# The first products of an encoder block on Trainium2: two beside the loading of x, or four

## Chip, core and metric

The kernel runs on one core of a Trainium2 chip. The metric is the device time of one execution in microseconds, taken as the median of several executions. TensorE (PE in the profile) multiplies, VectorE (DVE) and ScalarE (ACT) work on whole tiles of 128 partitions, GpSimd (POOL) can do such work too, and SyncE (SP) issues most transfers from main memory.

## What is computed

One layer of a bidirectional encoder, then a last norm, on 256 positions of width 2048. The start is all that matters here:

```python
h = rms_norm(x, norm1_g)           # x * rsqrt(mean(x*x) + eps) * g
proj = h @ w_in                    # 2048 -> 9632 columns
u_a, v_a, feat_b, gate_a, gate_b = split_cols(proj, ...)
y_a = sgu_mixer(u_a, v_a, ...)     # begins with gelu(v), gelu(u)
```

Behind it come a scan over 16 heads, two projections and a gated feed-forward part. All matrices are float32.

## The kernel before

x is held transposed: 16 tiles of 128 features x 256 positions, loaded two at a time into `xt` (256 KB each). The norm is applied late. Each tile of x is only multiplied by `norm1_g` (`split_scaled`, L176), and the products are multiplied by `rstd1` once it is known. For precision every operand is split into a rounded part and the rest: ACT writes the rounded part and DVE the difference. That holds for x (`h`, L177 on ACT and L178 on DVE, 128x256 each) and for the weights (`hl`, L223 and L224, 128x512 each).

The weights come as chunks: one load (`raw`, 256 KB) of four 128x128 tiles. A chunk costs one cast on ACT, one subtraction on DVE and eight matmuls, in four pairs of one 512-column and one 256-column matmul (L242, L246). A product over 2048 features is four chunks. A list of jobs says in which order the chunks run; `split_to` prepares a chunk, `load_to` issues loads, `advance` multiplies. Four `raw` buffers, four `hl` buffers and two banks of PSUM for products (`ps_mm`) are turned over, and a load is issued when the subtraction that read its buffer is done.

At the start `pair_up` interleaves the chunks of the first two products, so that each quarter of x is used for two products while the next one comes in (the loop at L479 to L486). In the same loop POOL squares x (L482) and DVE sums the squares (L484). A matmul with a matrix of ones (L490) then gives the sum over all features, from which DVE forms `rstd1` (L493 and `rsqrt`, seven small instructions). The products that wait for `rstd1` are held in `waiting` and passed to the Gelu afterwards. The vectors of all norms and scales come in one load, `colt` (184 KB, issued by ACT at L127), and the constants in another, `cst`; five small DVE instructions (L144 to L152) derive vectors from `colt` before anything else.

The order on each engine is the one in which the program issues its instructions, with small moves by the scheduler of the language.

Of the kernel before, what the change touches and what calls it, by code (L numbers as in the profile page):

```python
# [24 lines left out]
NP = RW // P  # L25
# [4 lines left out]
RK = 4  # L30
# [18 lines left out]
NFEAT = 4 + 3 * NP  # L49
# [8 lines left out]
COLS = {}  # L58
# [58 lines left out]
def hybrid_kernel(ctx: ExitStack, tc: tile.TileContext, xT, w_in, w_pa, w_pb, w_out, w_g, w_u, w_d,  # L117
                  cols, consts, lora, sgu_wT, sgu_b, out):
    nc = tc.nc
    V, A, PE, G = nc.vector, nc.scalar, nc.tensor, nc.gpsimd  # L120

    cpool = ctx.enter_context(tc.tile_pool(name="cpool", bufs=1))
    ps_mm = ctx.enter_context(tc.tile_pool(name="ps_mm", bufs=2, space=PSUM))
    ps_ms = ctx.enter_context(tc.tile_pool(name="ps_ms", bufs=1, space=PSUM))

    colt = cpool.tile([P, NCOLS], F32, name="colt")
    A.dma_start(colt, cols)  # L127
    cst = cpool.tile([P, NCONST], F32, name="cst")
# [12 lines left out]


    c0 = cpool.tile([P, NFEAT], F32, name="c0")
    V.tensor_tensor(out=c0, in0=colr("mu_p"), in1=colr("mu_n"), op=ALU.add)  # L144
    V.tensor_scalar(out=c0, in0=c0, scalar1=-1.0, scalar2=1.0, op0=ALU.mult, op1=ALU.add)
    wo, _ = COLS["w0_f"]
    hb = cpool.tile([P, 4 * NP], F32, name="hb")
    V.tensor_scalar(out=hb, in0=colt[:, wo:wo + 4 * NP], scalar1=0.5, scalar2=None, op0=ALU.mult)
    ka2 = cpool.tile([P, NP], F32, name="ka2")
    V.tensor_scalar(out=ka2, in0=colr("k_a"), scalar1=-1.0, scalar2=2.0, op0=ALU.mult, op1=ALU.add)  # L150
    rkh = cpool.tile([P, NP], F32, name="rkh")
    V.tensor_scalar(out=rkh, in0=colr("r_k"), scalar1=0.5, scalar2=None, op0=ALU.mult)  # L152
    nln2 = cpool.tile([P, 1], F32, name="nln2")
    V.memset(nln2, LN2)

# [3 lines left out]
    ones = con("ones")  # L159
# [16 lines left out]
    def split_scaled(dst, src, g):  # L176
        A.activation(dst[:, 0], src, AF.Copy, scale=g)  # L177
        V.scalar_tensor_tensor(out=dst[:, 1], in0=src, scalar=g, in1=dst[:, 0].bitcast(F32),  # L178
                               op0=ALU.mult, op1=ALU.subtract)


    jobs, raws, chunks = [], [], []
    ptr = dict(raw=0, hl=0, mm=0)
# [11 lines left out]
        jobs.append(job)  # L195
        return job

    def pair_up(n):

        order = [i + o for i in range(n) for o in (0, n)]  # L200
        at = {ri: i for i, ri in enumerate(order)}
        raws[:2 * n] = [raws[ri] for ri in order]
        first = sorted((c for c in chunks if c[1] < 2 * n), key=lambda c: at[c[1]])
# [12 lines left out]
    def split_to(i):  # L216
        while ptr["hl"] <= min(i, len(chunks) - 1):
            c = chunks[ptr["hl"]]
            load_to(c[1] + (pools["ahead"] if ptr["mm"] > 7 else 0))
            _, ri, s0, m, _ = c  # L220
            raw = raws[ri][3]
            hl = hl_p.tile([P, 2, HK, P], F32R, name="hl", tag="hl")
            A.copy(hl[:, 0, :m], raw[:, s0:s0 + m])  # L223
            V.tensor_tensor(out=hl[:, 1, :m], in0=raw[:, s0:s0 + m], in1=hl[:, 0, :m].bitcast(F32), op=ALU.subtract)  # L224
            c[4] = hl
            ptr["hl"] += 1

    def advance(n, ahead=HL_AHEAD):
        for _ in range(n):
            i = ptr["mm"]  # L230
            if i >= len(chunks):
                return
            split_to(i + ahead)
            job, ri, s0, m, hl = chunks[i]
            if job["ps"] is None:
                job["ps"] = ps_mm.tile([P, 512], F32, name="mm", tag="mm")
            ps = job["ps"]
            for j in range(m):
                k = raws[ri][1] + s0 + j
                a = job["act"](k)  # L240
                if job["wide"]:
                    PE.matmul(ps[:, 0:512], hl[:, 0, j], a.rearrange("p a t -> p (a t)"), start=(k == 0), stop=False)  # L242
                else:
                    PE.matmul(ps[:, 0:256], hl[:, 0, j], a[:, 0], start=(k == 0), stop=False)  # L244
                    PE.matmul(ps[:, 0:256], hl[:, 0, j], a[:, 1], start=False, stop=False)  # L245
                PE.matmul(ps[:, 0:256], hl[:, 1, j], a[:, 0], start=False, stop=(k == job["nk"] - 1))  # L246
            ptr["mm"] += 1
            if ptr["mm"] == job["last"]:
                job["done"](ps if job["wide"] else ps[:, 0:T])
# [12 lines left out]
    pools = dict(raw=ctx.enter_context(tc.tile_pool(name="raw", bufs=4)), ahead=2)  # L262
    hl_p = ctx.enter_context(tc.tile_pool(name="hl", bufs=4))
    ev = ctx.enter_context(tc.tile_pool(name="ev", bufs=2))
    drp = ctx.enter_context(tc.tile_pool(name="drp", bufs=1, space=bass.MemoryType.DRAM))
# [5 lines left out]
    h = [hp.tile([P, 2, T], F32R, name=f"h{k}") for k in range(KT)]  # L271
# [67 lines left out]
    ps_s = es_s.enter_context(tc.tile_pool(name="ps_s", bufs=2, space=PSUM))  # L339
# [7 lines left out]
    waiting = []  # L347

    def gelu(ps, outv, add):
        t = evac_sum(ev, ps)  # L350

        def then():
            V.tensor_tensor(out=t, in0=t, in1=rstd1, op=ALU.mult)
            A.activation(outv, t, AF.Gelu)
            if add == 0:
                A.copy(acc, outv)
            elif add is not None:
                V.tensor_tensor(out=acc, in0=acc, in1=outv, op=ALU.add)

        if waiting is None:  # L360
            then()
        else:
            waiting.append(then)
# [90 lines left out]
    def abreast(*gens):  # L454

        live = list(gens)
        while live:
# [5 lines left out]
                    live.remove(g)  # L463
            yield step

    pair_up(KT // RK)


    with tc.tile_pool(name="xin", bufs=1) as xin:
        XG = 2  # L470
        sq = [xin.tile([P, XG, T], F32, name=f"sq{g}") for g in range(KT // XG)]
        xt = [xin.tile([P, XG, T], F32, name=f"xt{g}") for g in range(KT // XG)]
        for g in range(KT // XG):
            nc.sync.dma_start(xt[g], xT[:, g * XG:(g + 1) * XG])
            if g % 2:
                load_to(g)
        load_to(8)
        nc.sync.dma_start(cst, consts)
        for g in range(KT // XG):  # L479
# [5 lines left out]
            if g % 2:  # L485
                advance(2, 1 if g < 7 else 0)  # L486
        advance(1, 1)
        sps = ps_ms.tile([P, 512], F32, name="ms", tag="ms")
        for j in range(XG):
            PE.matmul(sps[:, 0:T], ones, sq[0][:, j], start=(j == 0), stop=(j == XG - 1))  # L490
# [6 lines left out]
        waiting = None  # L497

    nc.sync.dma_start(wsT, sgu_wT)
    nc.sync.dma_start(bsb, sgu_b.to_broadcast([P, SW]))  # L500
    finish(last_v)
# [408 lines left out]
    for p in range(-1, NP):  # L910
# [12 lines left out]
        if p + 2 < NP:  # L923
            side.append((rwkv_rates(p + 2), RATES_Y))
            then.append((rwkv_operands(p + 2), OPER_Y))
        n = left() - (LAST if p == NP - 1 else 0)
# [11 lines left out]
                 ahead=RAW2 - 2)  # L938
# [82 lines left out]
    with tc.tile_pool(name="ev2", bufs=2, reuse_waits="tile") as ev2, \  # L1021
# [116 lines left out]
```

## Time and profile before

| | us |
|---|---|
| median of 3 runs | 1582.59 (1581.76 to 1582.97) |
| the profiled execution | 1567.25 |
| its span, first to last instruction | 1565.5 |
| PE busy in the span | 1531.2 (98%) |
| PE busy in the first 27 us | 15.14 |
| PE busy from 27 to 60 us | 33.00 |

All times of rows count from the start of the span. A row of a timeline gives the start, the length, engine, line, operation, output and inputs, the count of merged instructions, and in brackets the idle time of the engine before it with what ended that. Instructions of one engine overlap a little: a lone 128x512 subtraction is shown as 0.68 us, but two in a row start 0.60 us apart. So the cost in a full queue is read from starts, not from lengths. In the table of stretches the columns are busy time and instructions of each engine, then the granted clock, the share of the DMA engines in use, and GB/s.

### The profile page before, as it was taken

To read this page: it belongs to the slowest core of one execution; us is meant where nothing else is said; L and a number is where in the kernel's file an instruction comes from. 1 tells how busy PE (TensorE), PEld (TensorE's weight loads), DVE (VectorE), ACT (ScalarE), POOL (GpSimd) and SP (SyncE) were. 2 spreads that over 40 slices of the span, in tenths; PEclk is the share of its full clock that TensorE was granted. 3 is DMA by queue.
4 is the path that set the end of the run, shared out by engine and by line. 5 is a ranking of instruction groups with operands and counts; after the bars stand their busy time and mean duration, and the time that the engine had idled before them with its cause. 6 is when DMAs were issued, how large, how long until landed. Compare 5 with 4: busy or idle time off the path is not lost.

```text
span 1565.5 us, 35582 instructions
## 1 busy us (share of the span) xinstructions
PE 1531.2 (98%) x13420; PEld 1333.2 (85%) x13420; DVE 1222.2 (78%) x2500; ACT 922.6 (59%) x1920; POOL 37.9 (2%) x65
## 2 busy tenths in 40 slices
PE   6999999999999999999999999999999999999996
PEld 5888888888888878899998888888888888888885
DVE  8879998889898897687678777777787776555554
ACT  5667765665666655555556666666666665545452
POOL 2000000000000000000000000000000000000000
PEclk9999999999999999999999999999999999999998
DMA  6555553443443433597555555555555556666663
GB/s 230 195 181 177 166 160 126 132 144 120 135 140 116 139 100 124 161 316 240 187 182 188 194 190 189 189 192 190 190 189 189 190 191 191 189 191 190 190 190 100
DMA packets 151500, 273.72 MB, mean 175 GB/s; under 512 B 16928, under 2 KB 23200, under 8 KB 151328
## 3 DMA queue, kind: packets, MB, share of 16 engines
q1 hardware_dynamic: 148624, 263.91, 53.2%
q0 software_dynamic: 2560, 7.34, 1.4%
q8 instruction: 105, 1.72, 0.4%
q14 instruction: 67, 0.55, 0.1%
q10 hardware_dynamic: 144, 0.19, 0.0%
HBM read 265.09 MB, written 6.29 MB: 173 GB/s over the span
## 4 chain that ended last, share of the span: by engine, by line
PE 84%; issue 9%; DVE 4%; DMA 1%; ACT 1%; POOL 0%; SPq 0%; DVEq 0%; ACTq 0%; POOLq 0%
PE mm L242 45%; PE mm L246 26%; PE mm L244 3%; PE mm L245 3%; PE gp L669 1%; PE tp L717 1%; PE ms L541 1%; DVE hl L224 1%; DVE FQ L695 1%; PE tp L707 1%; PE cc L800 0%; DMA xt<-in_xT_dram 0%; PE tp L728 0%; DMA spill<-ev 0%; POOL spill L877 0%
## 5 line engine op out<-in xcount | busy, mean ns | idle before, releaser
L242 PE MATMUL mm<-h,hl 128*128 128x512 f32 x2624 | 935.7, 399 | 8.3 <-DVE h L178 7.6
L224 DVE TENSOR_TENSOR hl<-raw,hl 128x512 fp32r<-128x512 f32 x960 | 655.9, 689 | 231.0 <-ACT hl L223 227.3
L223 ACT CAST hl<-raw 128x512 fp32r<-128x512 f32 x960 | 594.7, 621 | 398.5 <-PE mm L246 284.9
L246 PE MATMUL mm<-h,hl 128*128 128x256 f32 x2624 | 733.3, 279 | 4.8 <-DVE hl L224 4.8
L242 PEld LDWEIGHTS mm<-h,hl 128*128 128x128 f32 x2624 | 493.2, 188 | 122.4 <-ACT hl L223 8.1
L246 PEld LDWEIGHTS mm<-h,hl 128*128 128x128 f32 x2624 | 495.0, 189 | 7.9 <-DVE hl L224 7.1
L242 PE MATMUL mm<-act,hl 128*128 128x512 f32 x660 | 228.8, 394 | 0.0
L246 PE MATMUL mm<-act,hl 128*128 128x256 f32 x704 | 195.3, 277 | 0.0
L242 PEld LDWEIGHTS mm<-act,hl 128*128 128x128 f32 x660 | 123.8, 188 | 28.7
L258 ACT COPY ev<-mm 128x256 f32<-128x256 f32 x180 | 67.1, 373 | 119.0 <-PE mm L246 118.7
L246 PEld LDWEIGHTS mm<-act,hl 128*128 128x128 f32 x704 | 132.4, 188 | 0.0
L259 DVE TENSOR_TENSOR ev<-mm,ev 128x256 f32<-128x256 f32 x180 | 75.9, 422 | 45.5 <-ACT ev L258 44.7
L246 PE MATMUL mm<-mg,hl 128*128 128x256 f32 x256 | 71.9, 281 | 0.0
L244 PE MATMUL mm<-mg,hl 128*128 128x256 f32 x256 | 71.7, 280 | 0.0
L245 PE MATMUL mm<-mg,hl 128*128 128x256 f32 x256 | 71.2, 278 | 0.0
L242 PE MATMUL mm<-ya,hl 128*128 128x512 f32 x128 | 48.2, 409 | 0.0
L244 PEld LDWEIGHTS mm<-mg,hl 128*128 128x128 f32 x256 | 48.1, 188 | 0.0
L245 PEld LDWEIGHTS mm<-mg,hl 128*128 128x128 f32 x256 | 48.1, 188 | 0.0
L246 PEld LDWEIGHTS mm<-mg,hl 128*128 128x128 f32 x256 | 48.1, 188 | 0.0
L1035 ACT ACTIVATE gt<-cp,colt 128x256 f32<-128x256 f32 x44 | 26.5, 603 | 19.1 <-DVE cp L1033 19.1
L246 PE MATMUL mm<-ybs,hl 128*128 128x256 f32 x128 | 36.2, 283 | 0.0
L245 PE MATMUL mm<-ybs,hl 128*128 128x256 f32 x128 | 36.2, 283 | 0.0
(285 smaller groups left out, 1523.6 us busy)
## 6 DMA issues: line engine op xcount, KB each, us to landing
raw<-in_w_in_dram SPq DMA_DIRECT2D x304, 256.0 KB, 3.0
raw<-in_w_g_dram SPq DMA_DIRECT2D x176, 256.0 KB, 3.1
raw<-in_w_u_dram SPq DMA_DIRECT2D x176, 256.0 KB, 2.9
raw<-in_w_d_dram SPq DMA_DIRECT2D x176, 256.0 KB, 2.9
raw<-in_w_out_dram SPq DMA_DIRECT2D x64, 256.0 KB, 3.0
raw<-in_w_pa_dram SPq DMA_DIRECT2D x32, 256.0 KB, 2.9
raw<-in_w_pb_dram SPq DMA_DIRECT2D x32, 256.0 KB, 4.7
spill<-ev POOLq DMA_DIRECT2D x32, 128.0 KB, 3.2
```

The source lines that it names most:

```text
L223: A.copy(hl[:, 0, :m], raw[:, s0:s0 + m])
L224: V.tensor_tensor(out=hl[:, 1, :m], in0=raw[:, s0:s0 + m], in1=hl[:, 0, :m].bitcast(F32), op=ALU.subtract)
L242: PE.matmul(ps[:, 0:512], hl[:, 0, j], a.rearrange("p a t -> p (a t)"), start=(k == 0), stop=False)
L244: PE.matmul(ps[:, 0:256], hl[:, 0, j], a[:, 0], start=(k == 0), stop=False)
L245: PE.matmul(ps[:, 0:256], hl[:, 0, j], a[:, 1], start=False, stop=False)
L246: PE.matmul(ps[:, 0:256], hl[:, 1, j], a[:, 0], start=False, stop=(k == job["nk"] - 1))
L258: A.copy(t, ps[:, 256:512])
L259: V.tensor_tensor(out=t, in0=ps[:, 0:256], in1=t, op=ALU.add)
L541: PE.matmul(ps[:, 0:T], bones, b[:, o], start=(o == 0), stop=(o == 1))
L669: PE.matmul(gps[hh][:, c * P:(c + 1) * P], BK[rows, d, c, hh:hh + 2, :].rearrange("p a b -> p (a b)"), AR[rows, d, c].rearrange("p a b -> ...
L695: V.copy_predicated(out=FQ2[qs, d, :, 1, :], mask=m2[qs, None, :].to_broadcast([32, NC, 32]), data=Gs[d][qs, q // 2, :, 0, b0:b0 + 32])
L1035: A.activation(gt, b[:, 1:T + 1], AF.Identity, scale=col("cw1", f), bias=col("cb", f))
```

## The change

Four products instead of two run side by side while x comes in. `line_up(4, 4)` takes the place of `pair_up(4)`; the third and fourth product borrow banks of PSUM (tags `sgt` and `sgm`) that are free until the gating stage. In this stage eight buffers (`rawx`) take the loads, and a load of a quarter of x is followed by the four chunks that use it. The squares are made by ACT, 128x512 each, in place of POOL; DVE still sums them. The scale of norm 1 comes in a load of its own (`g1t`, 16 columns), the whole `colt` only after half of x is in use, and the five small DVE instructions (`derive`) stand behind the norm. The matmul that sums the squares uses a matrix of ones made on the core (`on1`). Twelve 512-column matmuls of that constant by itself stand first on PE; nothing reads them. Results that wait for `rstd1` lie in four buffers (`evw`) instead of two.

```diff
+J0 = 4
+WARM = 12
...
+    g1t = cpool.tile([P, KT], F32, name="g1t")
+    A.dma_start(g1t, cols[:, 0:KT])
     colt = cpool.tile([P, NCOLS], F32, name="colt")
-    A.dma_start(colt, cols)
...
-    pair_up(KT // RK)
-
-
-    with tc.tile_pool(name="xin", bufs=1) as xin:
+    line_up(J0, KT // RK)
+
+
+    with tc.tile_pool(name="xin", bufs=1) as xin, tc.tile_pool(name="evw", bufs=J0) as evw, \
+            tc.tile_pool(name="rawx", bufs=2 * J0) as rawx:
...
+        warm = ps_ms.tile([P, 512], F32, name="ms", tag="ms")
+        for _ in range(WARM):
+            PE.matmul(warm, on1.bitcast(F32R), on1.bitcast(F32R)[:, None, :].to_broadcast([P, 4, P]), start=True, stop=True)
...
+        def squares(q):
+            for g in (2 * q, 2 * q + 1):
+                sn = sq if g == 0 else xin.tile([P, XG, T], F32, name="sn", tag="sn", bufs=2)
+                A.activation(sn, xt[g], AF.Square)
+                if g > 0:
+                    V.tensor_tensor(out=sq, in0=sq, in1=sn, op=ALU.add)
+
+        load_q(0)
+        load_q(1)
+        for q in range(NQ):
+            take(RK * q)
+            for i in range(J0):
+                c = J0 * q + i
+                split_to(c)
+                if i == 0:
+                    for k in range(RK * q + 1, RK * q + RK):
+                        take(k)
+                advance(1, 0)
+            load_q(q + 2)
+            if q == 1:
+                nc.sync.dma_start(colt, cols)
+            if q == NQ - 1:
+                pools["raw"] = main_raw
+                load_to(J0 * NQ + 2)
+            squares(q)
         nc.sync.dma_start(cst, consts)
-        for g in range(KT // XG):
-            for j in range(XG):
-                split_scaled(h[g * XG + j], xt[g][:, j], col("norm1_g", g * XG + j))
-            G.tensor_tensor(out=sq[g], in0=xt[g], in1=xt[g], op=ALU.mult)
-            if g > 0:
-                V.tensor_tensor(out=sq[0], in0=sq[0], in1=sq[g], op=ALU.add)
-            if g % 2:
-                advance(2, 1 if g < 7 else 0)
+        pools["ps"] = ps_next
         advance(1, 1)
```

What DVE does first, before the change (`h` are tiles of x, `hl` chunks of weights, `sq` sums of squares; the number behind a name tells tiles apart):

```order
L144 TENSOR_TENSOR c0_67<-colt_64 128x28
L148 TENSOR_SCALAR hb_70<-colt_64 128x32
L150 TENSOR_SCALAR ka2_72<-colt_64 128x8
L145 TENSOR_SCALAR c0_67<-c0_67 128x28
L152 TENSOR_SCALAR rkh_74<-colt_64 128x8
L178 SCALAR_TENSOR_TENSOR h0_100<-xt0_181,colt_64,h0_100 128x256
L178 SCALAR_TENSOR_TENSOR h1_101<-xt0_181,colt_64,h1_101 128x256
L178 SCALAR_TENSOR_TENSOR h2_102<-xt1_182,colt_64,h2_102 128x256
L178 SCALAR_TENSOR_TENSOR h3_103<-xt1_182,colt_64,h3_103 128x256
L224 TENSOR_TENSOR hl_227<-raw_191,hl_227 128x512
L224 TENSOR_TENSOR hl_230<-raw_193,hl_230 128x512
```

And with the change:

```order
L489 MEMSET on1_175 128x128
L185 SCALAR_TENSOR_TENSOR h0_96<-xt0_190,g1t_64,h0_96 128x256
L185 SCALAR_TENSOR_TENSOR h1_97<-xt0_190,g1t_64,h1_97 128x256
L231 TENSOR_TENSOR hl_221<-raw_200,hl_221 128x512
L185 SCALAR_TENSOR_TENSOR h2_98<-xt1_191,g1t_64,h2_98 128x256
L185 SCALAR_TENSOR_TENSOR h3_99<-xt1_191,g1t_64,h3_99 128x256
L231 TENSOR_TENSOR hl_239<-raw_203,hl_239 128x512
L517 TENSOR_TENSOR sq_198<-sq_198,sn_286 128x512
L231 TENSOR_TENSOR hl_251<-raw_205,hl_251 128x512
L231 TENSOR_TENSOR hl_263<-raw_207,hl_263 128x512
L185 SCALAR_TENSOR_TENSOR h4_100<-xt2_192,g1t_64,h4_100 128x256
```

The small vectors have left the front, the first chunk is prepared before the third tile of x, and four chunks instead of two follow each four tiles of x.

What DVE does where `rstd1` is formed (`ev` are products that wait for it, `ms` the sum over features), with the change:

```order
L266 TENSOR_TENSOR ev_477<-mm_266,ev_477 128x256
L231 TENSOR_TENSOR hl_552<-raw_496,hl_552 128x512
L545 TENSOR_SCALAR s1_513<-ms_510 128x256
L171 TENSOR_SCALAR rstd1_75<-s1_513 128x256
L174 TENSOR_TENSOR t1_514<-rstd1_75 128x256
L175 SCALAR_TENSOR_TENSOR t1_514<-t1_514,s1_513 128x256
L176 SCALAR_TENSOR_TENSOR rstd1_75<-t1_514,rstd1_75 128x256
L231 TENSOR_TENSOR hl_557<-raw_545,hl_557 128x512
L174 TENSOR_TENSOR t1_514<-rstd1_75 128x256
L231 TENSOR_TENSOR hl_570<-raw_550,hl_570 128x512
```

Here `hl_552` is chunk 19 and `hl_557` chunk 20, counted from the first. Before the change the same chain stands behind chunk 10, with two held products; now five are held when it ends. Behind this stage the rows of all five engines are the same in both kernels.

## Rows read from the trace of the kernel before

**Rows 1.** Page: the span
```profile
span 1565.5 us, 35582 instructions
```
**Rows 2.** Stretches: before 27 us, from there to 60, and all behind 40
```profile
0.00:27.00 27.00, 15.14 (x60) 10.98 (x61) 22.96 (x40) 14.00 (x28) 9.63 (x12) 1.00 0.67 225
27.00:60.00 33.00, 33.00 (x191) 28.96 (x190) 26.30 (x53) 20.56 (x41) 0.00 (x0) 1.00 0.65 220
...
40.00:1565.50 1525.50, 1503.06 (x13288) 1310.92 (x13287) 1187.81 (x2436) 899.60 (x1875) 28.30 (x53) 1.00 0.55 173
```
**Rows 3.** Waits of PE in the first 46 us: total, times, longest
```profile
PE mm L242 <- DVE h L178: 7.6, 2, 7.3
PE mm L246 <- DVE hl L224: 4.2, 5, 1.2
```
**Rows 4.** Timeline of DVE
```profile
0.90 0.55 DVE L278 MEMSET fp<- 128x258 f32 x2
4.61 0.94 DVE L144 TENSOR_TENSOR c<-colt 128x28 f32<-128x28 f32 x1 [3.16 <-DMA colt<-in_cols_dram]
...
9.54 3.90 DVE L178 SCALAR_TENSOR_TENSOR h<-xt,colt,h 128x256 fp32r<-128x256 f32 x4
13.37 1.52 DVE L224 TENSOR_TENSOR hl<-raw,hl 128x512 fp32r<-128x512 f32 x1
...
22.30 1.28 DVE L224 TENSOR_TENSOR hl<-raw,hl 128x512 fp32r<-128x512 f32 x2
23.50 0.87 DVE L178 SCALAR_TENSOR_TENSOR h<-xt,colt,h 128x256 fp32r<-128x256 f32 x2
24.30 0.68 DVE L484 TENSOR_TENSOR sq<-sq,sq 128x512 f32<-128x512 f32 x1
...
27.50 0.41 DVE L259 TENSOR_TENSOR ev<-mm,ev 128x256 f32<-128x256 f32 x1
27.83 0.68 DVE L224 TENSOR_TENSOR hl<-raw,hl 128x512 fp32r<-128x512 f32 x1
...
30.47 0.43 DVE L168 SCALAR_TENSOR_TENSOR t<-t,s 128x256 f32<-128x256 f32 x1
```
**Rows 5.** Timeline of POOL
```profile
4.48 2.07 POOL L482 TENSOR_TENSOR sq<-xt 128x512 f32<-128x512 f32 x2 [4.03 <-DMA xt<-in_xT_dram]
```
**Rows 6.** Timeline of ACT
```profile
4.61 1.70 ACT L177 ACTIVATE h<-xt,colt 128x256 fp32r<-128x256 f32 x4 [1.93 <-DMA colt<-in_cols_dram]
6.22 0.60 ACT L223 CAST hl<-raw 128x512 fp32r<-128x512 f32 x1
```
**Rows 7.** ACT's squares later on, by line: count, then ns min/median/max
```profile
L421 ACT ACTIVATE sqv<-vu x7: 400/414/418, 66.5 to 73.4; 128x256 f32<-128x256 f32 x7
```
**Rows 8.** Timeline of PE
```profile
8.96 0.58 PE L246 MATMUL mm<-h,hl 128*128 128x256 f32 x1 [0.93 <-DVE hl L224]
...
10.62 0.63 PE L242 MATMUL mm<-h,hl 128*128 128x512 f32 x1
...
13.18 0.49 PE L242 MATMUL mm<-h,hl 128*128 128x512 f32 x1
...
26.43 1.13 PE L490 MATMUL ms<-sq,cst 128*128 128x256 f32 x4
27.21 0.47 PE L246 MATMUL mm<-h,hl 128*128 128x256 f32 x1
...
28.56 0.39 PE L242 MATMUL mm<-h,hl 128*128 128x512 f32 x1
...
39.82 0.39 PE L242 MATMUL mm<-h,hl 128*128 128x512 f32 x1
```
**Rows 9.** Stretches with transfers at work, with few, and again at work
```profile
8.00:12.00 4.00, 3.07 (x11) 2.66 (x11) 3.96 (x6) 2.92 (x6) 2.54 (x2) 1.00 0.98 327
14.00:15.00 1.00, 0.08 (x2) 0.06 (x1) 1.00 (x2) 1.00 (x3) 0.63 (x2) 1.00 0.28 107
27.00:28.00 1.00, 1.00 (x7) 0.90 (x6) 1.00 (x3) 0.71 (x3) 0.00 (x0) 1.00 1.01 412
```

More of the change, by code (lines that the diff above doesn't have):

```diff
@@ L143, in hybrid_kernel, with derive @@
     c0 = cpool.tile([P, NFEAT], F32, name="c0")
-    V.tensor_tensor(out=c0, in0=colr("mu_p"), in1=colr("mu_n"), op=ALU.add)
-    V.tensor_scalar(out=c0, in0=c0, scalar1=-1.0, scalar2=1.0, op0=ALU.mult, op1=ALU.add)
-    wo, _ = COLS["w0_f"]
     hb = cpool.tile([P, 4 * NP], F32, name="hb")
-    V.tensor_scalar(out=hb, in0=colt[:, wo:wo + 4 * NP], scalar1=0.5, scalar2=None, op0=ALU.mult)
     ka2 = cpool.tile([P, NP], F32, name="ka2")
-    V.tensor_scalar(out=ka2, in0=colr("k_a"), scalar1=-1.0, scalar2=2.0, op0=ALU.mult, op1=ALU.add)
     rkh = cpool.tile([P, NP], F32, name="rkh")
-    V.tensor_scalar(out=rkh, in0=colr("r_k"), scalar1=0.5, scalar2=None, op0=ALU.mult)
+    def derive():
+        V.tensor_tensor(out=c0, in0=colr("mu_p"), in1=colr("mu_n"), op=ALU.add)
+        V.tensor_scalar(out=c0, in0=c0, scalar1=-1.0, scalar2=1.0, op0=ALU.mult, op1=ALU.add)
+        wo, _ = COLS["w0_f"]
+        V.tensor_scalar(out=hb, in0=colt[:, wo:wo + 4 * NP], scalar1=0.5, scalar2=None, op0=ALU.mult)
+        V.tensor_scalar(out=ka2, in0=colr("k_a"), scalar1=-1.0, scalar2=2.0, op0=ALU.mult, op1=ALU.add)
+        V.tensor_scalar(out=rkh, in0=colr("r_k"), scalar1=0.5, scalar2=None, op0=ALU.mult)
     nln2 = cpool.tile([P, 1], F32, name="nln2")
@@ L196, in push, with line_up @@
         return job
-    def pair_up(n):
-        order = [i + o for i in range(n) for o in (0, n)]
+    def line_up(w, n):
+        order = [i + n * o for i in range(n) for o in range(w)]
         at = {ri: i for i, ri in enumerate(order)}
-        raws[:2 * n] = [raws[ri] for ri in order]
-        first = sorted((c for c in chunks if c[1] < 2 * n), key=lambda c: at[c[1]])
+        raws[:w * n] = [raws[ri] for ri in order]
+        first = sorted((c for c in chunks if c[1] < w * n), key=lambda c: at[c[1]])
         for i, c in enumerate(first):
@@ L218, in split_to @@
             c = chunks[ptr["hl"]]
-            load_to(c[1] + (pools["ahead"] if ptr["mm"] > 7 else 0))
+            load_to(c[1] + (pools["ahead"] if ptr["mm"] >= J0 * KT // RK else 0))
             _, ri, s0, m, _ = c
@@ L235, in advance @@
             if job["ps"] is None:
-                job["ps"] = ps_mm.tile([P, 512], F32, name="mm", tag="mm")
+                job["ps"] = pools["ps"](job)
             ps = job["ps"]
@@ L262, in hybrid_kernel @@
     pools = dict(raw=ctx.enter_context(tc.tile_pool(name="raw", bufs=4)), ahead=2)
+    ps_next = lambda job: ps_mm.tile([P, 512], F32, name="mm", tag="mm")
+    pools["ps"] = ps_next
     hl_p = ctx.enter_context(tc.tile_pool(name="hl", bufs=4))
@@ L349, in gelu @@
     def gelu(ps, outv, add):
-        t = evac_sum(ev, ps)
+        t = evac_sum(pools["wait"], ps)
         def then():
@@ L464, in abreast @@
             yield step
-    pair_up(KT // RK)
-    with tc.tile_pool(name="xin", bufs=1) as xin:
+    line_up(J0, KT // RK)
+    with tc.tile_pool(name="xin", bufs=1) as xin, tc.tile_pool(name="evw", bufs=J0) as evw, \
+            tc.tile_pool(name="rawx", bufs=2 * J0) as rawx:
         XG = 2
-        sq = [xin.tile([P, XG, T], F32, name=f"sq{g}") for g in range(KT // XG)]
+        NQ = KT // RK
+        pools["wait"] = evw
+        pools["ps"] = lambda job: next(
+            (ps_s.tile([P, 512], F32, name="mm", tag=tag) for i, tag in ((2, "sgt"), (3, "sgm")) if job is jobs[i]),
+            None) or ps_next(job)
+        main_raw, pools["raw"] = pools["raw"], rawx
+        on1 = xin.tile([P, P], F32, name="on1")
+        V.memset(on1, 1.0)
+        warm = ps_ms.tile([P, 512], F32, name="ms", tag="ms")
+        for _ in range(WARM):
+            PE.matmul(warm, on1.bitcast(F32R), on1.bitcast(F32R)[:, None, :].to_broadcast([P, 4, P]), start=True, stop=True)
@@ L472, in hybrid_kernel, with load_xt, load_q @@
         xt = [xin.tile([P, XG, T], F32, name=f"xt{g}") for g in range(KT // XG)]
-        for g in range(KT // XG):
+        def load_xt(g):
             nc.sync.dma_start(xt[g], xT[:, g * XG:(g + 1) * XG])
-            if g % 2:
-                load_to(g)
-        load_to(8)
-        nc.sync.dma_start(cst, consts)
-        for g in range(KT // XG):
-            for j in range(XG):
-                split_scaled(h[g * XG + j], xt[g][:, j], col("norm1_g", g * XG + j))
-            G.tensor_tensor(out=sq[g], in0=xt[g], in1=xt[g], op=ALU.mult)
-            if g > 0:
-                V.tensor_tensor(out=sq[0], in0=sq[0], in1=sq[g], op=ALU.add)
-            if g % 2:
-                advance(2, 1 if g < 7 else 0)
+        def load_q(q):
+            if q < NQ:
+                load_xt(2 * q)
+                load_to(J0 * q)
+                load_xt(2 * q + 1)
+                load_to(J0 * q + J0 - 1)
@@ new lines, in take @@
+        def take(k):
+            split_scaled(h[k], xt[k // XG][:, k % XG], g1t[:, k:k + 1])
+        sq = xin.tile([P, XG, T], F32, name="sq")
+        def squares(q):
[22 more added lines that the diff above has]
+            squares(q)
@@ L487, in hybrid_kernel @@
+        nc.sync.dma_start(cst, consts)
+        pools["ps"] = ps_next
         advance(1, 1)
@@ L489, in hybrid_kernel @@
         for j in range(XG):
-            PE.matmul(sps[:, 0:T], ones, sq[0][:, j], start=(j == 0), stop=(j == XG - 1))
+            PE.matmul(sps[:, 0:T], on1, sq[:, j], start=(j == 0), stop=(j == XG - 1))
         s1 = xin.tile([P, T], F32, name="s1")
@@ L497, in hybrid_kernel @@
         waiting = None
+        derive()
+    pools["wait"] = ev
     nc.sync.dma_start(wsT, sgu_wT)
```

## The prediction

> **What bounds the kernel now.** I read the stretches first, then PE's waits, then the timelines of the first 40 us. PE is busy in all 33.00 us from 27 to 60 and in 1503.06 of the 1525.5 us behind 40; in the first 27 it is busy for 15.14 [rows 2]. So PE bounds nearly the whole span of 1565.5 us [rows 1], and what an edit of the start can win lies in the first 27 us. There PE waits for DVE alone: 7.6 us for tiles of x (7.3 of them before its first matmul) and 4.2 us for weights [rows 3]. DVE itself is busy for 22.96 of those 27 us [rows 2]: it is the bound of this stage.
>
> Two causes lie behind that. DVE idles until 4.61, when `colt` lands, and then works through five small instructions before the first tile of x [rows 4]. And it is slow while POOL squares: four tiles of x take 3.90 us and one subtraction 1.52, at 9.54 and 13.37, whereas later two subtractions start 1.20 us apart from what follows (22.30 to 23.50, 0.60 each) and two tiles of x 0.80 (23.50 to 24.30, 0.40 each) [rows 4]. POOL's squares begin at 4.48, when the first x has landed [rows 5], and fill 9.63 us [rows 2].
>
> **A ruler.** I number chunks of weights as PE takes them; from chunk 16 on it is the same work in both kernels and the same order. Before, chunk 8 starts at 28.56 and chunk 16 at 39.82 [rows 8]: 1.41 us per chunk, hiccups included (eight matmuls without one would be 1.39). PE has no gap behind that, so the time at which chunk 17 starts, 39.82 + 1.41 = 41.23, less the time at which the changed kernel starts it, is the gain.
>
> **The change, part by part.**
>
> Warm matmuls. The constant is set behind DVE's two memsets, which end at 1.45 [rows 4], so PE starts near 1.7. Before, PE worked without a gap from 8.96, and up to 13.18 a pair of matmuls of 768 columns took 0.64 us (10.62 to 13.18, four pairs); behind that a pair takes 0.35 [rows 8]. That is the lower of the two clock levels, 1.2 GHz, and then 2.4; the column of the granted clock reads 1.00 throughout, so I go by the pairs. Twelve matmuls of 512 columns at two thirds of 0.64 are 5.1 us and end at 6.8; with the clock rising 4.2 us after the start, as it did here, at 6.5. I take 6.7. The first real operands come no earlier (next part), so these matmuls cost at most 0.7 us and buy the full clock for chunk 0.
>
> Scale and order at the front. ACT can start on x at 4.48 to 4.61 [rows 5, 6] if `g1t` is there; `colt`, of 184 KB, landed by 4.61, and I take that for the 8 KB load as well, with a start at 4.48 if it comes sooner. The Trainium skill speaks against such a load: DMA: Bandwidth & Descriptors, section "Rules for kernel authors", says that transfers under 64 KB are mostly overhead and should be merged. By the same page's fixed cost of about 2 us the scale would be there by about 3, an estimate, ahead of x, and the sum would not move; no row here has a load this small. ACT needs 0.40 for a tile of x ((6.22 - 4.61) / 4) and 0.60 for a cast [rows 6]: h0, h1 and the first cast end at 6.0, and DVE's part of chunk 0 at 6.6. Then a square (two of 0.41 at half its width [rows 7], or 0.60 like the cast: I take 0.60) and h2, h3 on ACT to 7.4, on DVE to 7.9. So chunk 0 ends near 8.3, chunk 1, whose subtraction ends at 8.6, near 9.9; DVE's sum of squares pushes chunk 2's subtraction to 9.8, and from there on PE is the last.
>
> The stage from 9.9 on, by engine, for a quarter of x with its four chunks:
> PE 4 x 1.41 = 5.6 us. DVE 4 x 0.40 + 4 x 0.60 + 2 x 0.60 (sums) = 5.2, since nothing on POOL disturbs it. ACT 4 x 0.40 + 4 x 0.60 + 2 x 0.60 = 5.2, with squares at 0.82 5.6. Transfers: six of 0.262 MB; at the 327 GB/s of 8 to 12 us [rows 9] 0.80 each, 4.8 us. With eight buffers a load waits for the subtraction eight chunks back, never the late one. So PE is the bound, by little. Chunks 2 to 15 take 14 x 1.41 = 19.7 us: chunk 16 starts at 29.6. The check from the other side: the load of chunk 15 is the 24th, lands at 4.5 + 23 x 0.80 = 22.9; DVE reaches its subtraction after 16 x 0.40 + 22 x 0.60 = 19.6 us of work from 5.0 and 1.9 of waits in the first quarter, and ends it at 26.5. PE wants it at 28.2.
>
> Behind it. The matmul with ones now stands behind chunk 16 with PE full: 0.78 us (26.43 to 27.21 [rows 8]), where it lay in gaps before. Chunk 17 starts at 29.6 + 1.4 + 0.8 = 31.8. That is 9.4 us sooner.
>
> What DVE still owes. From chunk 15 to chunk 23 it has 8 subtractions (4.8), one sum (0.6), five additions of products at 0.33 (27.50 to 27.83 [rows 4]; 1.65), the five small instructions moved here (0.85 at 0.17), `rsqrt` and what leads to it (eight at 0.43 to 0.46; 3.5), and five products by `rstd1` (1.65): 13.1 us, to 39.6. PE wants chunk 23 at 31.8 + 6 x 1.41 = 40.2. The cover is half a microsecond, and each one by which DVE is later than I think costs as much. For this I take off 0.4: **a gain of 9.0 us**. `colt` is issued behind chunk 15's load, lands near 24 and is first read at about 27.8. The two big loads `wsT` and `bsb` stand ahead of chunk 20's load, as they stood ahead of chunk 11's; DVE wants that chunk at 34. POOL's squares go at no gain of their own, other than DVE's pace, and the added buffers cost no time.
>
> **The rivals.**
>
> A, the transfers bound the stage. For it: six transfers of 4.8 us stand against 5.6, and the mean of the first 27 us is only 225 GB/s [rows 2]. Against: that mean holds stretches like 14 to 15 us at 107 GB/s, when loads waited for buffers [rows 9]. At 225 GB/s a transfer is 1.16 us, chunk 15 lands at 31.2 and ends near 33.6, chunk 17, with `colt` ahead of it, starts at 36.6: gain 4.6, 1578.0 us.
>
> B, the warm matmuls do not raise the clock, or it falls again before the operands come. Then PE runs pairs at 0.64 from 6.7 for 4.2 us more: 1.6 chunks in that time, where I count three by 11.1. 1.3 chunks are 1.9 us: gain 7.1, 1575.5. For it: no row shows such matmuls. Against: before, with waits of up to 1.2 us [rows 3] behind 13.18, the pairs stayed fast.
>
> C, slower. DVE's slow rows were not POOL's doing but that of the transfers, which ran at a share of 0.98 from 8 to 12 us [rows 9]; the change keeps them running, and doubles what DVE has to do. At 0.97 and 1.5 us DVE would need 16 x 0.97 + 22 x 1.5 = 48.5 us to chunk 15: chunk 17 at some 56, 15 us later than now: 1598. It decides from a subtraction of 1.0 us on. Against: at 14 to 15 us the transfers are at 0.28 and DVE is still inside the slow row of 13.37; at 27 to 28 they are at 1.01 and a subtraction (27.83) takes 0.68 [rows 4, 9]. The Trainium skill excludes it: SBUF — State Buffer, section "SBUF: two separate sides", says that engine ports and DMA ports do not contend and only DVE and GpSimd share a port pair, one blocking the other. By that rule its chance is nil; by the rows alone I would leave it 5 in 100, and put 3.
>
> D, the gain is given back: something behind 40 us waits for no engine of this stage. PE's idle time there is 22.4 us in all [rows 2], so there is room, but the order is the same and PE pulls the loads itself. No change: 1582.6.
>
> **How the numbers follow.** The sum is made on the profiled execution, 1567.25 us; the median of the runs lies 15.3 us above it, a difference that I take to stay. So 1582.6 - 9.0 = 1573.6, and a profiled span near 1556.5. Chances: the forecast 65 in 100 (1572.5 to 1575), B 15, A 12, D 5, C 3. The best case is sixteen chunks without a gap from 6.5: chunk 17 at 6.5 + 17 x 1.39 + 0.8 = 30.9, gain 10.3, and the runs before scatter by 0.6: low end 1571.7. The high end takes in A: 1578.0. That leaves out C, D and a worse A. A measurement can tell about 0.2%, 3.2 us, from no change. Faster by more: the forecast, B and most of A, 0.90. Same: D and the rest of A, 0.06. Slower: C and an unknown, 0.04.
>
> **What the profile after would show.** Subtractions at 0.68 us and tiles of x at 0.47 from the first one on; if not, C. The warm matmuls from 1.7 to 6.7 with the last ones twice as fast, and pairs of chunk 0 at 0.35; if not, B. PE without gaps over 0.2 us from about 10 on, chunk 16 at 29.6 and chunk 17 at 31.8. Waits of ACT for `raw` in that stretch would mean A. A wait of PE for DVE between 34 and 42 us would mean that DVE's debt of 13.1 us was under-counted. What would make the forecast wrong most easily is the chain ACT, DVE, PE of each chunk: three engines within 8% of each other leave little room for a bad order.

## The result: 22 us, of which 9 were forecast

| us | before | changed |
|---|---|---|
| median | 1582.78 (4 runs, 1581.76 to 1584.15) | 1560.63 (4 runs, 1557.87 to 1573.84) |
| profiled execution | 1567.25 | 1557.87 |

The ratio is 0.9875 (95% interval 0.9838 to 0.9913), some 22 us, well over twice the gain that was forecast, and the time lies below the range. The changed runs lie at two levels: three at 1557.87 to 1560.64 and one at 1573.84. And the profiled executions differ by 9.4 us only. So the table holds two questions: did the start do what was forecast, and where do the other 13 us come from?

Page of the changed kernel:

```profile
span 1556.1 us, 35601 instructions
```

Its span was forecast near 1556.5. The stretches of the changed kernel (busy time and instructions of PE, PEld, DVE, ACT and POOL, granted clock, DMA share, GB/s):

```profile
0.00:27.00 27.00, 25.14 (x126) 20.96 (x127) 21.99 (x45) 22.19 (x45) 0.20 (x4) 1.00 0.94 333
12.00:16.00 4.00, 4.00 (x24) 3.23 (x23) 4.00 (x8) 4.00 (x10) 0.00 (x0) 1.00 1.06 407
27.00:60.00 33.00, 33.00 (x190) 28.76 (x189) 28.75 (x67) 21.56 (x45) 0.00 (x0) 1.00 0.55 179
40.00:1556.10 1516.10, 1493.86 (x13234) 1302.63 (x13232) 1182.07 (x2427) 895.05 (x1870) 28.28 (x53) 1.00 0.55 173
```

Against [rows 2], PE is busy for 25.14 of the first 27 us, where it was for 15.14; 4.6 of them are the matmuls of the constant. From 27 to 60 it still has no gap. Behind 40 it is idle for 22.2 us, where it was for 22.4.

Waits of the changed kernel in the first 60 us (total, times, longest), those of PE and two of ACT; they answer to [rows 3]:

```profile
ACT hl L230 <- DMA raw<-in_w_in_dram: 3.8, 7, 1.3
...
PE ms L493 <- DVE on L489: 1.6, 1, 1.6
...
ACT h L184 <- DMA g1t<-in_cols_dram: 1.2, 1, 1.2
...
PE mm L253 <- DVE hl L231: 0.2, 1, 0.2
```

PE waits 1.6 us for the constant and then 0.2 for DVE, where it waited 11.8. ACT's 3.8 us for weights cost nothing, since PE doesn't wait. Timeline of PE in the changed kernel, which answers to [rows 8]:

```profile
1.64 4.76 PE L493 MATMUL ms<-on 128*128 128x512 f32 x12 [1.64 <-DVE on L489]
6.24 0.39 PE L249 MATMUL mm<-h,hl 128*128 128x512 f32 x1
...
8.51 0.39 PE L253 MATMUL mm<-h,hl 128*128 128x256 f32 x1 [0.22 <-DVE hl L231]
...
29.52 0.39 PE L249 MATMUL mm<-h,hl 128*128 128x512 f32 x1
...
30.90 1.03 PE L542 MATMUL ms<-sq,on 128*128 128x256 f32 x4
31.58 0.58 PE L249 MATMUL mm<-h,hl 128*128 128x512 f32 x1
```

The matmuls of the constant end at 6.24 and the first real one follows at once, at 0.39 us for 512 columns: the full clock. Chunk 16 starts at 29.52 (forecast 29.6) and chunk 17 at 31.58 (31.8). DVE in the changed kernel, against [rows 4]:

```profile
4.43 0.89 DVE L185 SCALAR_TENSOR_TENSOR h<-xt,g1t,h 128x256 fp32r<-128x256 f32 x2 [2.85 <-ACT h L184]
...
14.85 1.28 DVE L231 TENSOR_TENSOR hl<-raw,hl 128x512 fp32r<-128x512 f32 x2
...
25.25 0.69 DVE L231 TENSOR_TENSOR hl<-raw,hl 128x512 fp32r<-128x512 f32 x1
...
38.83 0.68 DVE L231 TENSOR_TENSOR hl<-raw,hl 128x512 fp32r<-128x512 f32 x1
```

No slow rows are left: two subtractions take 1.28 us at 14.85, though the transfers run at 407 GB/s there. Chunk 15's subtraction (25.25) ends at 25.9, chunk 23's (38.83) at 39.5. ACT in the changed kernel, against [rows 6]:

```profile
3.89 0.91 ACT L184 ACTIVATE h<-xt,g1t 128x256 fp32r<-128x256 f32 x2 [1.22 <-DMA g1t<-in_cols_dram]
...
5.43 0.63 ACT L515 ACTIVATE sq<-xt 128x512 f32<-128x512 f32 x1
```

The small load `g1t` landed at 3.89; ACT's first square began at 5.43 and what follows it at 5.96.

So the start did what was forecast. The other 13 us are not in it.

### The profile page after: what moved, and what is told of

Read it like the earlier page. It is cut to its first block, busy times and chain, and to the rows that moved or that the text cites. A ratio compares the mean times of both kernels' runs of the same rounds, so it can differ in the third digit from the quotient of the medians.

```text
span 1556.1 us, 35601 instructions
## 1 busy us (share of the span) xinstructions
PE 1532.0 (98%) x13432; PEld 1335.0 (86%) x13432; DVE 1215.4 (78%) x2501; ACT 925.1 (59%) x1928; POOL 28.5 (2%) x57
## 4 chain that ended last, share of the span: by engine, by line
PE 85%; issue 9%; DVE 4%; ACT 1%; DMA 1%; POOL 0%; SPq 0%; DVEq 0%; ACTq 0%; POOLq 0%
PE mm L249 46%; PE mm L253 26%; PE mm L251 3%; PE mm L252 3%; PE gp L723 1%; PE tp L771 1%; PE ms L595 1%; DVE FQ L749 1%; PE tp L761 1%; DVE hl L231 1%; PE cc L854 0%; PE tp L782 0%; POOL spill L931 0%; DMA spill<-ev 0%; ACT hl L230 0%
```

## Two theories, and where the traces differ

**The first theory:** the change's own gain is the 9 us of the start. The other 13 come from something far behind the start that has two levels in either kernel, and the profiled execution of before (1567.25) happened to have the good one, its timed runs the bad one. **Its rival:** the kernel before takes 1582 us, its profiled execution was an exception, and the change itself brought 22. The first two runs repeat the two kernels unchanged.

**e1, the kernel before again.**

> The kernel before, unchanged. Theory 1: the start gains 9.4 us in every execution, and the other 12 us between the medians are a second level, some 14 us higher, into which an execution of either kernel falls, whatever the change; then some executions of this kernel lie near 1567 (as its profiled one did) and some near 1582, and those of the changed kernel 9 to 10 us below either. Theory 2: the change itself takes a further 12 to 15 us out of the executions that are not profiled; then this kernel stays at 1581 to 1584 in every round and the changed one at 1558 to 1562.

All eleven executions took 1582.22 to 1584.98 us (median 1583.12), the profiled one 1583.15. That no execution fell on the good level spoke for the rival, but it gave what was missing: a profile at 1583.

**e2, the changed kernel again.**

> The changed kernel, as it is. Theory 1 (two levels, whatever the kernel): executions near 1558 to 1561 and near 1573, in about the proportion that the kernel before shows between 1567 and 1582 on this chip. Theory 2 (the change removes the further time): all near 1558 to 1562, with 1573 an exception, while the kernel before stays at 1582. Both expect a span of 1556 to 1557 in the lower level, PE on chunk 16 at 29.5 us.

Two levels again: 1559.66, 1559.77, 1560.09, 1560.89, and 1573.94, 1574.09; the profiled execution was at 1574.09. So each kernel now has a profile at either level. I compared them stretch by stretch. One stretch of 480 us in which PE has no gap, 820 to 1300, of the kernel before, first its profile at 1567.25:

```profile
820.00:1300.00 480.00, 480.00 (x2771) 419.79 (x2770) 379.72 (x739) 291.35 (x562) 0.00 (x0) 1.00 0.58 190
```

then e1, its profile at 1583.15:

```profile
820.00:1300.00 480.00, 480.00 (x2719) 416.22 (x2718) 374.86 (x726) 285.83 (x551) 0.00 (x0) 1.00 0.57 186
```

then the changed kernel at 1557.87:

```profile
820.00:1300.00 480.00, 480.00 (x2772) 419.58 (x2771) 378.93 (x736) 291.12 (x562) 0.00 (x0) 1.00 0.59 190
```

and e2, the same kernel at 1574.09:

```profile
820.00:1300.00 480.00, 480.00 (x2719) 416.35 (x2718) 374.10 (x722) 285.36 (x552) 0.00 (x0) 1.00 0.57 187
```

PE is busy throughout in all four, the granted clock reads 1.00 in all four, and yet two do 2771 or 2772 matmuls and two 2719, 1.9% fewer. PE's timeline shows how. The kernel before at 1567.25, the first and the fifth start of a 512-column matmul (four pairs lie between them):

```profile
1000.03 0.40 PE L242 MATMUL mm<-h,hl 128*128 128x512 f32 x1
...
1001.42 0.40 PE L242 MATMUL mm<-h,hl 128*128 128x512 f32 x1
```

and e1, the same kernel at 1583.15:

```profile
1000.04 0.40 PE L242 MATMUL mm<-h,hl 128*128 128x512 f32 x1
...
1001.45 0.40 PE L242 MATMUL mm<-h,hl 128*128 128x512 f32 x1
```

Four pairs take 1.39 us in the one and 1.41 in the other. From all starts, by their finer time stamps, the pairs repeat as 350, 343 ns in the one (mean 346.7) and as 349, 350, 361 in the other (mean 353.3). Either pace holds without one exception from the last interruption, a matmul with ones (at 817 and 819 us here), to 1540. Let me call them the short and the long pace. The long one costs (1540 - 820) / 0.3533 x 0.0066 = 13.5 us. Counted by matmuls, the stretch from the 9000th to the 13000th takes:

```
                      9000th    13000th   between
before,  1567.25      798.25    1483.98    685.7
e1,      1583.15      800.40    1498.94    698.5
changed, 1557.87      787.13    1472.28    685.2
e2,      1574.09      789.60    1487.52    697.9
```

It is 12.8 us longer in e1 than in the first profile of before, and 12.7 in e2 than in the first profile of the changed kernel. So the level belongs to the execution and not to the one kernel or the other, and the rival fell here, though the repeated times alone had favoured it. What the change did to how often an execution has the lower level is taken up with e7 and e9. Of the 15.9 us by which e1's span is longer than that of [rows 1], 12.8 are the pace in this stretch; 2.2 lie ahead of the 9000th matmul and 0.9 behind the 13000th.

About two of those 2.2 us have a cause that the start of e1 shows, first in the stretch

```profile
0.00:27.00 27.00, 14.65 (x53) 11.20 (x54) 22.57 (x39) 13.73 (x28) 10.13 (x12) 0.89 0.68 217
```

and then on PE's timeline in e1:

```profile
24.42 0.63 PE L242 MATMUL mm<-h,hl 128*128 128x512 f32 x1
...
25.06 0.63 PE L242 MATMUL mm<-h,hl 128*128 128x512 f32 x1
...
28.42 1.02 PE L490 MATMUL ms<-sq,cst 128*128 128x256 f32 x4
```

A pair takes 0.64 us at 24.42, and the granted clock is 0.89 over the stretch, where it was 1.00 in [rows 2]. From 22 to 27 alone it is 0.50, the level of 1.2 GHz:

```profile
22.00:27.00 5.00, 5.00 (x16) 3.96 (x17) 5.00 (x11) 0.66 (x2) 0.00 (x0) 0.50 0.91 267
```

Ahead of it PE had waited for DVE several times, 0.65 us at 20.41 and 0.36 at 21.80 the last. The matmul with ones starts at 28.42, where it did at 26.43 [rows 8]. So what the prediction held against B, that the pairs stayed fast behind waits of up to 1.2 us, is true of one execution of this kernel and not of another.

## The parts of the start, one at a time

Each of these runs undoes one part of the changed kernel. Since the level jumps by 13 us, times are compared at the same level. At the short pace the changed kernel's median is 1560.09 (seven runs, three of the first result and four of e2); at the long one it took 1573.84 to 1574.09. The ruler turns out to be coarser than it was taken for. Chunk 17 starts at 31.58 in the first profile of the changed kernel, but in e2 at

```profile
32.67 0.58 PE L249 MATMUL mm<-h,hl 128*128 128x512 f32 x1
```

and in e11 (below; the same start, and the short pace behind 820 us) at

```profile
32.87 0.58 PE L249 MATMUL mm<-h,hl 128*128 128x512 f32 x1
```

So single profiles of one and the same start differ by 1.3 us in it, whatever their pace later on; why was not followed. A smaller difference in chunk 17 shows nothing, and the times of the runs decide.

**e3, without the matmuls of the constant.**

```diff
-WARM = 12
+WARM = 0
```

> The changed kernel without the twelve matmuls of the constant (WARM = 0; nothing reads them). Theory: PE's first pairs take 0.64 us until some 4 us after the first operands, chunk 17 starts about 1.9 us later than 31.6 (at 33 to 33.7), span 1557.5 to 1558.5 in the lower level. Rival: DVE and ACT, not PE, set the pace of the first quarter, so the slow pairs are hidden; chunk 17 within 0.4 us of 31.6 and span near 1556.3.

Five runs at the short pace have a median of 1561.61, 1.5 us more; the sixth took 1574.87 (ratio to before 0.9882, 0.9859 to 0.9906). PE's timeline in e3:

```profile
6.17 0.79 PE L249 MATMUL mm<-h,hl 128*128 128x512 f32 x1 [6.17 <-ACT hl L230]
...
7.28 0.63 PE L249 MATMUL mm<-h,hl 128*128 128x512 f32 x1
...
11.01 0.40 PE L249 MATMUL mm<-h,hl 128*128 128x512 f32 x1
...
32.83 0.58 PE L249 MATMUL mm<-h,hl 128*128 128x512 f32 x1
```

The first product starts at 6.17, so in the changed kernel the constant's matmuls delayed it by 0.07 us. Here PE runs at the lower clock until about 10.9. Chunk 17 starts at 32.83, earlier than the 33 to 33.7 expected, later than the rival's 31.6, and inside the spread above, so the price goes by the runs: 1560.71 to 1562.84 here against 1557.87 to 1560.89, 1.5 us between the medians with a small overlap. The mechanism of rival B, slow first pairs unless the clock is up, is real; its price was put at 1.9.

**e4, squares on POOL again.**

```diff
-                A.activation(sn, xt[g], AF.Square)
+                G.tensor_tensor(out=sn, in0=xt[g], in1=xt[g], op=ALU.mult)
```

> The changed kernel with the squares of x back on POOL. Theory (POOL's squares hold DVE up): subtractions of 1.5 us and tiles of x of 0.9 us as long as POOL squares, 8 x 1.2 us of it, of which DVE loses about 5.5 us; it had 1.7 us in hand at chunk 15, so chunk 17 starts 3 to 5 us later, span 1559 to 1561. Rival (the transfers slowed DVE before, or nothing of the kind): DVE at 0.68 and 0.47 as in the changed kernel, ACT relieved of 5 us, span 1555.5 to 1556.5.

Median of five runs at the short pace 1562.49, 2.4 us more, and one of 1578.17 (ratio 0.9891, 0.9864 to 0.9918). The profile, at the long pace, has chunk 17 at 35.16,

```profile
35.16 0.58 PE L249 MATMUL mm<-h,hl 128*128 128x512 f32 x1
```

2.3 to 3.6 later than in the three above (3 to 5 were expected). DVE's timeline in e4:

```profile
17.65 1.27 DVE L185 SCALAR_TENSOR_TENSOR h<-xt,g1t,h 128x256 fp32r<-128x256 f32 x1
18.84 1.52 DVE L231 TENSOR_TENSOR hl<-raw,hl 128x512 fp32r<-128x512 f32 x1
```

and POOL's at that time:

```profile
16.61 3.21 POOL L515 TENSOR_TENSOR sn<-xt 128x512 f32<-128x512 f32 x2 [2.96 <-DVE sq L517]
```

One tile of x takes 1.27 us and one subtraction 1.52 while POOL squares, where a lone one takes about 0.47 and 0.68 without it. In the changed kernel the transfers are as busy and DVE is not slow. That settles rival C: the slow rows of [rows 4] were POOL's doing. The rule of the Trainium skill (SBUF — State Buffer, "SBUF: two separate sides") that DVE and GpSimd share a port pair and transfers contend with neither agrees with both traces.

**e6, two products side by side.**

```diff
-J0 = 4
+J0 = 2
```

> The changed kernel with two products side by side (J0 = 2, so two waiting results and four load buffers), all else as changed. Theory (four products give PE work to cover DVE and ACT): a quarter of x costs DVE 4 x 0.40 + 4 x 0.60 = 4.0 us against 2.8 on PE, so PE waits for DVE; chunk 8 starts near 22 and chunk 17 near 35, 3 to 4 us later than with four, span 1559 to 1560.5 on the faster level. Rival (the gain came from POOL, the scale and the clock, not from four products): chunk 17 within 1 us of 31.6.

The four lower runs took 1562.88 to 1564.09, 3.1 us more (ratio 0.9907, 0.9876 to 0.9938). PE's waits in the first 60 us of e6:

```profile
PE mm L253 <- DVE hl L231: 2.3, 5, 0.7
...
PE mm L249 <- DVE h L185: 0.3, 1, 0.3
PE mm L249 <- ACT hl L230: 0.2, 1, 0.2
```

With two products there is half the work per tile of x, and PE waits 2.8 us. Chunk 17 starts at

```profile
37.54 0.39 PE L249 MATMUL mm<-h,hl 128*128 128x512 f32 x1
```

where 35 was expected, 4.9 us later than in e2; at the end of the two profiled executions (1577.70 and 1574.09) 3.6 of them are left. The load buffers follow `J0` and are four instead of eight, the buffers of waiting results two instead of four, so this is not the price of the number of products alone: by e8, below, the buffers cost 1.6 us beside four products.

**e7, one load for all vectors,** first in ACT's queue, with no tile `g1t`:

```diff
-    g1t = cpool.tile([P, KT], F32, name="g1t")
-    A.dma_start(g1t, cols[:, 0:KT])
     colt = cpool.tile([P, NCOLS], F32, name="colt")
+    A.dma_start(colt, cols)
+    g1t = colt
...
-            if q == 1:
-                nc.sync.dma_start(colt, cols)
```

> The changed kernel with the whole table of vectors loaded first again, and the scale taken from it. Theory: ACT starts at 4.4 to 4.7 instead of 3.9, but PE is busy with the constant until 6.3, so chunk 17 comes 0.2 to 0.7 us later, span 1556.3 to 1556.8 on the faster level. Rival: the first load holds the whole chain up, chunk 17 more than 1 us later.

All five runs took 1572.25 to 1573.88, the long pace (ratio 0.9942, 0.9929 to 0.9955). At the same level that is 0.5 us less than the changed kernel, where the theory expected 0.2 to 0.7 more and the rival over 1. ACT's first tile of x starts at 4.94 instead of 3.89, and DVE's five small instructions are back at the front, but chunk 17 starts at 32.25, inside the spread. The small load thus buys nothing that these runs show; where its earlier landing is lost was not followed. The Trainium skill's advice (DMA: Bandwidth & Descriptors, "Rules for kernel authors") to merge transfers under 64 KB agrees with that; the fixed cost of about 2 us, which the same page fitted on loads issued from GpSimd, does not give the landing of this one from ACT's queue, 3.1 us behind the issue. But why did no run have the short pace? That question led to e9.

**e8, four load buffers.**

```diff
-            tc.tile_pool(name="rawx", bufs=2 * J0) as rawx:
+            tc.tile_pool(name="rawx", bufs=J0) as rawx:
```

> The changed kernel with four load buffers instead of eight in the first stage. Theory: a load then waits for the subtraction four chunks back, 5.5 us ahead of its use, and lands in 3 to 5 us; the transfers just keep up, chunk 17 0.5 to 3 us later, span 1557 to 1559 on the faster level. Rival: no difference (transfers have room), within 0.3 us.

Five runs at the short pace have a median of 1561.70, 1.6 us more, and one took 1574.38 (ratio 0.9882, 0.9859 to 0.9905). The stretch in e8:

```profile
0.00:27.00 27.00, 24.94 (x124) 20.29 (x124) 19.34 (x39) 20.31 (x41) 0.20 (x4) 1.00 0.80 253
```

253 GB/s instead of 333: the loads wait for buffers, and PE waits 1.3 us for what they bring.

## What sets the pace

**e5, the kernel before with small extra matmuls.** If the pace is set by how the stream restarts behind an interruption, an interruption of another length should change it. Behind each product of the feed-forward part, 44 times, stands one matmul of 16, 32, ... 128 columns whose result nobody reads:

```diff
+        ps_k = ctx.enter_context(tc.tile_pool(name="ps_k", bufs=1, space=PSUM))
+        kt = ps_k.tile([P, 512], F32, name="kt")
...
+            n = 16 * (1 + f % 8)
+            if n:
+                PE.matmul(kt[:, 0:n], h2[0][:, 0, 0:P], h2[0][:, 0, 0:n], start=True, stop=True)
```

> The kernel before with one extra small matmul (16 to 128 columns in turn, read by nothing) after each of the 44 pairs of products of the feed-forward part. Theory (the two levels are two repeating patterns of PE's pairs, 346.7 or 353.3 ns a pair, into which an unbroken stream falls after its last interruption): the trace shows stretches of both paces between the kicks, changing only at kicks, and a time between 1567 and 1586. Rival (the pace is given for the execution, by the chip or the data): one pace from 820 to 1300 us, kicks or not.

Eight runs, 1577.9 to 1579.6, median 1578.43 (ratio 0.9981, 0.9962 to 1.0), and in the trace the pace changes at these matmuls and nowhere between them. Mean of six pairs ahead of and behind each of the first eight, in ns:

```
columns   16     32     48     64     80     96    112    128
ahead   353.3  353.3  346.7  346.7  346.7  353.3  353.3  346.7
behind  353.3  346.7  346.7  346.7  353.3  353.3  346.7  353.3
```

The next rounds of eight repeat this. Behind 32, 48, 64 and 112 columns the stream runs at the short pace, behind the other four at the long one. Each length met the same pace ahead of it every time, so that the outcome may depend on that pace too. (The profile of e11, below, has one case of the other kind: ahead of the 32 columns the stream ran at the short pace there, and so it did behind them.)

**e9, the kernel before with 64 bytes more.** e7 is the one variant of the changed kernel without the tile `g1t`, 64 bytes of each partition, and it never had the short pace. So the kernel before got an unused tile of that size at that place:

```diff
+    pad = cpool.tile([P, KT], F32, name="pad")
+    V.memset(pad, 0.0)
```

> The kernel before with one unused tile of 16 columns (64 bytes a partition) ahead of all others, set once by DVE, in the place where the change puts its small load; nothing else. Theory (the small tile moves every later tile by 64 bytes, and that, by a few ns in the last interruption before the long stream, decides between the paces of 346.7 and 353.3 ns): most executions 12 to 14 us below the kernel before, at 1568 to 1571, and the interval ahead of 816 us that takes 425 ns takes 416. Rival (the order or time of the start decides): as the kernel before, 1581 to 1584.

Of twelve runs eight took 1568.21 to 1570.55 and four 1581.69 to 1584.18 (median 1569.64; ratio 0.9974, 0.9938 to 1.001). On the same chip 6 of 23 runs of the kernel before were below 1571, in all its other runs 1 of 49 (without the first profiled execution, 1567.25). The variants of the changed kernel with the tile (the kernel itself, e2, e3, e4, e6, e8) had the short pace in 26 of 34 runs. The stretch in e9's profile shows that it is the same thing:

```profile
820.00:1300.00 480.00, 480.00 (x2771) 419.80 (x2770) 380.65 (x741) 291.00 (x562) 0.00 (x0) 1.00 0.58 190
```

So the odds go with the tile, from either side (added in e9, removed in e7). How sure is that? 8 of 12 against 6 of 23 would come by chance about 3 times in 100, the ratio's interval takes in 1, the odds of the kernel before also differ between chips, and neither edit is the tile alone: e9 adds a small instruction on DVE, e7 changes the loads of the front. The second thing that was expected of e9 makes it likelier. The first interval between two matmuls behind the next to last interruption (817.5 us in e9) takes 425 ns in all five profiles without the tile (before, e1, e5, e7, e10) and 416 to 418 in all eight with it, e9 among them. So the tile does touch PE's timing there. But this interval doesn't decide the pace: behind 425 the first profile of the kernel before had the short pace and e1 the long one, behind 416 the first profile of the changed kernel the short one and e2 the long. The tile doesn't fix the pace, then. Whether it acts by the addresses behind it or otherwise was not tried apart.

**e10 and e11, both kernels steered.** If the pace is all that is left, matmuls of 32, 48 and 64 columns behind the second to fourth feed-forward product should put both kernels on the short one, and the difference should be the 9 us of the start. The edit is that of e5 with another line, in the kernel before (e10) and in the changed one (e11):

```diff
+            n = {1: 32, 2: 48, 3: 64}.get(f)
```

> The kernel before with three of the small matmuls only, of 32, 48 and 64 columns, after the second, third and fourth pair of products of the feed-forward part (read by nothing). Theory (a fixed pattern, left and entered by interruptions of a given length): from 353.3 the first leads to 346.7, the others keep it; all executions at 1568.5 to 1571, none at 1582. Rival (chance at each interruption): both levels as before.

> The changed kernel with the same three small matmuls. Theory: the executions that would be at 1574 come down to the others, all at 1559 to 1562; those that enter the stream at 346.7 already may be moved by the first matmul and brought back by the third. Rival: both levels remain, 1560 and 1574.

e10: twelve runs, 1568.78 to 1571.23, median 1569.21 (ratio to before 0.9935, 0.9909 to 0.9961). e11: six runs, 1559.58 to 1561.45, median 1560.18 (0.9879, 0.9842 to 0.9916). Neither had a run at the upper level. PE's timeline of e10 around the first of these matmuls:

```profile
838.13 0.40 PE L242 MATMUL mm<-h,hl 128*128 128x512 f32 x1
...
839.19 0.40 PE L242 MATMUL mm<-h,hl 128*128 128x512 f32 x1
...
839.88 0.18 PE L1052 MATMUL kt<-h 128*128 128x32 f32 x1
839.91 0.47 PE L242 MATMUL mm<-h,hl 128*128 128x512 f32 x1
...
840.35 0.40 PE L242 MATMUL mm<-h,hl 128*128 128x512 f32 x1
...
841.39 0.39 PE L242 MATMUL mm<-h,hl 128*128 128x512 f32 x1
```

Three pairs take 1.06 us ahead of it (838.13 to 839.19) and 1.04 behind it (840.35 to 841.39); it costs 0.11 itself (839.53, the start of the pair ahead of it, to 840.35 are 0.81 in the finer stamps, for two pairs of 0.35). So this execution came out of its start on the long pace, and was put on the short one. With the pace equal, the change is worth 1569.21 - 1560.18 = 9.0 us; drawing anew from these 12 and 6 runs, 95% of the differences lie between 7.8 and 9.8. e11 is the version to keep: none of its six runs is near 1574. At 26 in 34 that would happen by chance one time in five, so that the small matmuls hold the pace rests on e10 (12 of 12, against 6 of 23) and on e5.

## Why the prediction was right in the start and wrong in the total

**Right, the gain.** 9.0 us were forecast, and 9.0 were measured with both kernels on one pace. At the long pace it is 1582.8 - 1574.0 = 8.8, at the short one without the small matmuls 1568.1 (six runs) - 1560.1 = 8.0, on different chips, and between the first two profiles 9.4. So the gain is 8 to 9.5 us, and that it came out at 9.0 to the tenth is luck. The mechanism held: PE's waits for DVE are gone, and DVE's slow rows with them. The ruler, chunk 17, gave 41.23 - 31.58 = 9.65, before the 0.4 that was taken off for DVE's debt. DVE ended chunk 23's subtraction at 39.5 (forecast 39.6), PE did not wait, and so that 0.4 was not needed. In its place the first profile of the changed kernel had the quickest start of the three: chunk 17 was forecast at 31.8 and came at 31.58 there, but at 32.67 and 32.87 in the others.

**The step that failed** is one half sentence: the median lies 15.3 us above the profiled execution, "a difference that I take to stay". It did not stay. It was 13 us of pace and some 2 us of other things, and the change moved most executions to the pace that the profile of before already had, probably by a tile of 64 bytes. The changed kernel's usual time then lies by its profile: 1560.6 against 1557.87. The difference, larger than the whole forecast gain and far larger than the 0.6 by which the runs scattered, should have been a term of the sum with bounds: from staying, 1573.6, to vanishing, 1567.25 - 9.0 = 1558.3. Those two are near the two levels that were then measured, 1574 and 1560.

**The terms, one by one.** The constant's matmuls ended at 6.24 (6.7) and raised the clock; the price of leaving them out is some 1.5 (1.9 by B), probably because the first chunks do not wait for PE alone. Transfers were better than taken: six of 0.262 MB in 3.9 us at 407 GB/s, 0.65 each, instead of 0.80, which leaves nothing of rival A; the 225 GB/s of [rows 2] were indeed loads that waited for buffers: in the first 27 us SyncE waited 12.6 us for DVE's subtractions in the kernel before, 0.9 in the changed one, and 8.4 in e8. A square on ACT costs 0.53 (5.43 to 5.96), not 0.60, and DVE's rows are the undisturbed ones from the first on, which is probably why chunk 15's subtraction ended 0.6 us early. The scale landed at 3.89, earlier than the 4.48 taken from `colt`, but e7 finds no gain in that. Rival D is out too: PE's idle time behind 40 us is unchanged, and nothing was given back.

**Which part carries the gain?** Going back to two products costs 3.1 us, to POOL's squares 2.4, to four buffers 1.6, to a cold start 1.5, to one load nothing. These do not add up to 9 and need not, since the parts cover each other and the order of the front was not undone alone.

## What to carry to other kernels

Look at how the profiled execution stands to the timed runs before anything is forecast: a difference larger than their scatter is a second level of the kernel, and a change may move it by accident. Count the instructions of the busiest engine in a long stretch without gaps and compare two profiles; a level that busy time and clock don't show is found there. A mark in a single profile, such as the start of chunk 17, can move by 1 us between executions of one start, so take several before a difference of that size is read from it. And measure a small gain with that level pinned in both kernels, as e10 and e11 do, or the level is taken for the gain.

## What was not expected of the hardware

A stream of pairs of a 512-column and a 256-column matmul on PE, without waits and at a granted clock of 1.00, runs at one of two paces, 346.7 or 353.3 ns a pair, and keeps it for 700 us until something interrupts it. Behind one extra matmul of 32, 48, 64 or 112 columns came the short pace, behind one of 16, 80, 96 or 128 the long one, the same each time (e5). With 64 bytes more per partition the odds were 8 in 12 instead of 6 in 23 on one chip (e9), and one interval at an interruption was 416 to 418 ns instead of 425 in every profile. Why two paces exist at all, and what picks one, stays open.
